# Second attention of a two-layer streaming encoder: keys on the partitions, maxima from a score pass of their own, query groups outside heads, output projection beside the next group

## The chip, the cores and the metric

One NeuronCore of one Trainium2 chip runs the whole program. The metric is the device time of one execution in microseconds (us), the median of several runs; lower is better. The engines are named as in the profile: PE (TensorE matmuls; PEld is its weight loads), DVE (VectorE), ACT (ScalarE), POOL (GpSimd) and SP (SyncE, which only issues DMAs here).

## The reference, cut to what matters

Two layers run on 2048 prompt tokens and 32 sample tokens, width 1024. Layer 0 (pooling mixer and sliding-window attention) and layer 1's input projection are the same before and after, but for the form in which layer 1's queries, keys and running sums are stored. What changes is layer 1's "forgetting attention" over the prompt (16 heads of 64) and the output projection behind it:

```python
cum_t = jnp.cumsum(logf, axis=1).transpose(0, 2, 1)          # running log-forget sums
bias  = ci[..., None] - cum_t[:, :, None, :]                 # c[query] - c[key]
s = jnp.einsum('nqhd,nkhd->nhqk', q, k) * ATTN_SCALE + bias  # per head, causal
p = jax.nn.softmax(jnp.where(mask, s, -jnp.inf), axis=-1)
out = jnp.einsum('nhqk,nkhd->nqhd', p, v)
y = x + (out * jax.nn.silu(gate)) @ w_out
```

Every product is computed to nearly fp32 accuracy by splitting an operand into a rounded part (hi) and the rest (lo). A split is two instructions: one engine rounds hi, another computes lo = value - hi.

## The kernel before, in words

The program is written in Python as one order of instructions. A planner then lays out each engine's stream ahead of time: it takes the written order as priority and an estimated timeline of when operands and buffers are ready, so an engine's stream can differ from the written order (matmuls of the output projection stand in PE's stream ahead of the last value products). At run time each engine works its own stream in order.

The stages: layer 0's projection, layer 0's attention with its output projection, layer 1's input projection with the sample's attention, and, as the last stage, the code of the change. There the loop runs over heads outside and over four groups I of 512 queries inside (`seq`).

`load_head` brings one head's operands for half of the tokens: qs (query hi over lo, 128 rows), ka (key hi over lo), kb (lo over hi) and vhl (value hi | lo) by POOL's DMA queue, and cb (the running sums, copied to all 128 partitions) by SP's.

`scores` has queries on the partitions. For each block of 128 queries and each piece of up to 1024 keys it issues two matmuls per 512 keys (ka, then kb: together all four hi/lo products), one small bf16 matmul for the causal mask, then one DVE instruction (L1053) that reads the scores in PSUM, adds cb, writes the sum to SBUF (pr) and returns the row's minimum (the scores are negated). ACT (L1058) takes the exponential of the whole row with the minimum as its bias and returns the row's sum.

`values` needs the probabilities with keys on the partitions, so PE transposes every 128x128 block (L1077) into PSUM (pt). The block is split: for three blocks of five ACT rounds hi from pt and DVE computes lo from pt (PSUM) and ph (SBUF); for two of five ACT copies pt to SBUF (pf), DVE rounds hi and POOL computes lo (`PM`, `PS`). Two matmuls per block (L1070) add vhl times ph and vhl times pl into pa. At the end of a group ACT copies one half of pa (L1093) and DVE adds the other (L1094).

`finish`, once per pair of heads and group, makes reciprocals of the row sums, transposes them, multiplies with the gate sg (DVE) and the result op (POOL, L1109), and stores to m1T by SP. `weave` spreads the next group's score pieces among a group's value blocks.

The output projection comes behind all heads: `load_wo` splits w_out's eight row tiles, `halves` loads 128 tokens of m1T and splits them, and `out1` (L1196) issues 2 x 24 matmuls of 512 columns per token tile, a DVE addition of the residual and a store.

Of the kernel before, what the change touches and what calls it, by code (L numbers as in the profile page):

```python
# [34 lines left out]
CW = 256  # L35


def f32(ap):
    return ap.bitcast(F32)
# [3 lines left out]
def hybrid_step_kernel(ctx: ExitStack, tc: tile.TileContext, *args):  # L43
# [34 lines left out]
    qT = dram([16, 2, HD, NTOK], "qT")  # L78
    kT = dram([16, 2, HD, NTOK], "kT")
# [3 lines left out]
    cT = dram([256, P], "cT")  # L83
# [21 lines left out]
    maskb = ctile([P, P], "maskb", BF16)  # L105
    with pool_of(name="setup", bufs=1) as setup:
# [4 lines left out]
        nc.vector.tensor_copy(maskb, mask)  # L111

# [24 lines left out]
    def rstd_bits(ss, np_, count):  # L137
        """as rstd_of, for one column and without a table: a first guess from the exponent's bits, then Newton"""
# [26 lines left out]
    def flush(n=0):  # L165
        """issue the stores that wait, but for the last n"""
# [4 lines left out]
    # ------------------------------------------------------------------  # L171
    # one layer's input projection, h^T held as exact hi/lo parts
    # ------------------------------------------------------------------
    class Proj:
# [13 lines left out]
        def at(self, which, tok, n):  # L188
            """hi (0) or lo (1) part of h^T for tokens [tok, tok + n): [P, KT, n]"""
# [59 lines left out]
        def prefetch(self, plan, fast=False):  # L249
            """the column groups in the order of use; the next one's weights are loaded ahead"""  # L250
# [49 lines left out]
        def turns(self, new=None):  # L300
            """the turn that waits, one step behind the arithmetic it needs"""
# [4 lines left out]
        def head_norm(self, src, np_, nh, gB, eng):  # L306
            """src: [np, nh, 64] (PSUM or SBUF) -> normalized, scaled tile [np, nh, 64]"""
# [13 lines left out]
    def turn(pt, ev, o, t0, h0, npair, dstT):  # L321
        """normalized heads [P, 2 token tiles, npair x 2 heads x 64] -> exact hi / lo parts, transposed"""
# [6 lines left out]
        for hh in range(2):  # L329
            for w in range(2):  # L330
                store(dstT[h0 + hh:h0 + 2 * npair:2, w, :, t0 * P:(t0 + 2) * P].rearrange("h d t -> d h t"),
                      f32(hl[hh * HD:(hh + 1) * HD, w]))
# [98 lines left out]
        # ALiBi with the chunk mask, keys = 128 before the tile and its own 128  # L431
# [11 lines left out]
        # the sample's keys, values and queries for the sliding window, hi / lo parts  # L443
# [123 lines left out]
    def out_proj(pp, pool, lhs, wo, xres, dst, n, eng):  # L567
        """lhs: for 128 tokens (hi, lo) APs [P, KT, 128]; for the sample one AP [P, KT, 64]"""
# [180 lines left out]
    # ------------------------------------------------------------------  # L749
    # layer 1, input projection  # L750
    # ------------------------------------------------------------------
    late = ctx.enter_context(pool_of(name="late", bufs=1))
    mhs = late.tile([P, KT, 2 * NS], F32R, name="mhs", tag="mhs")
    with ExitStack() as es:
# [38 lines left out]
        # log forget gates and their running sums  # L793
        with pool_of(name="lf", bufs=1) as lf:
# [28 lines left out]
            def running_sums(src_h, nt, dst, tag):  # L823
                """src_h: [P, 16, nt] with positions t*128+p; dst: DRAM [16*nt, 128]"""
# [13 lines left out]
                for j in range(0, n, P):  # L838
# [5 lines left out]
                    nc.sync.dma_start(dst[j:j + m, :], o)  # L844
# [411 lines left out]
```

## Time and profile before

| what | value |
|---|---|
| median of 3 runs | 2676.89 us (2674.86 to 2678.17) |
| profiled execution, its span | 2675.6 us |
| first score matmul of the changed stage | 1639.5 us |
| last value product; from here only the output projection | 2506.9 us |
| PE / DVE / ACT / POOL busy, whole span | 97% / 60% / 44% / 43% |

A busy time is the union of an engine's instructions. PE's instructions overlap each other (a matmul's recorded duration is longer than the distance to the next), so PE's rates are read from the chain of waits, where a run of matmuls stands as one piece with its count. The mean of a group of instructions is the recorded duration of one; back to back, DVE and ACT instructions overlap by about a tenth of a microsecond.

### The profile page before, as it was taken

What the parts mean: (1) busy time and instruction counts of PE and PEld (TensorE: products, weight loads), DVE (VectorE), ACT (ScalarE), POOL (GpSimd) and SP (SyncE); (2) the same over time, 40 slices, a digit from 0 to 9 for tenths busy, and PEclk for the clock granted to TensorE, in tenths of its full rate; (3) what the DMA queues carried; (4) which work ended last, traced back from release to release, by engine and by line L of the source; (5) the groups of instructions that cost most, each with busy time, mean ns of one, the idle gap of its engine ahead of it and who ended that gap; (6) DMA issues with size and microseconds to landing.
All of it is one profiled execution on the core that took longest, in us unless ns stands there. A gap on an engine that the chain in (4) does not pass through costs nothing. (4 is left out here: it accounts for less than half of the span.)

```text
span 2675.6 us, 47345 instructions
## 1 busy us (share of the span) xinstructions
PE 2586.7 (97%) x17259; PEld 2345.5 (88%) x17259; DVE 1604.6 (60%) x3847; ACT 1166.4 (44%) x2424; POOL 1149.9 (43%) x1583
## 2 busy tenths in 40 slices
PE   6999999799998999999999999999999999999999
PEld 6999999688887999999999998887888878877787
DVE  7650244778765115554553324889988988888521
ACT  5321111556554122222222114777777777777310
POOL 4454240455534434554554422555555555553100
PEclk9999999799998999999999999999999999999999
DMA  6342110976738443445555316544354455443642
GB/s 187 101 110 88 44 47 23 211 185 169 181 100 266 161 159 97 105 111 132 144 146 139 94 62 162 145 113 122 97 148 120 102 120 141 111 103 90 194 149 75
DMA packets 314120, 338.14 MB, mean 126 GB/s; under 512 B 32311, under 2 KB 263887, under 8 KB 313886
## 3 DMA queue, kind: packets, MB, share of 16 engines
q1 hardware_dynamic: 233550, 242.82, 31.6%
q0 software_dynamic: 76320, 87.98, 15.1%
q10 hardware_dynamic: 4016, 4.31, 0.5%
q8 instruction: 136, 2.23, 0.4%
q14 instruction: 98, 0.80, 0.1%
HBM read 203.05 MB, written 132.06 MB: 125 GB/s over the span
## 5 line engine op out<-in xcount | busy, mean ns | idle before, releaser
L271 PE MATMUL pm<-whl,h 128*128 128x256 f32 (+1 forms) x5760 | 713.7, 283 | 6.3 <-ACT h L155 3.1
L271 PEld LDWEIGHTS pm<-whl,h 128*128 128x128 f32 x5760 | 694.9, 190 | 7.9 <-ACT h L155 3.5
L296 PE MATMUL pm<-h,whl 128*128 128x384 f32 (+2 forms) x2880 | 472.3, 322 | 0.0
L296 PEld LDWEIGHTS pm<-h,whl 128*128 128x128 f32 x2880 | 455.3, 188 | 1.8
L158 POOL TENSOR_TENSOR pl<-pf,ph 128x512 fp32r<-128x512 f32 (+3 forms) x270 | 303.6, 1127 | 263.5 <-DVE ph L157 253.2
L1058 ACT ACTIVATE pr<-pr,mnf 128x128 f32<-128x128 f32 (+15 forms) x256 | 309.6, 1211 | 61.6 <-DVE mnf L1053 60.6
L1077 PE MATMUL pt<-ident,pr 128*128 128x128 f32 x2176 | 323.3, 274 | 5.5 <-DVE pl L158 5.4
L1077 PEld LDWEIGHTS pt<-ident,pr 128*128 128x128 f32 x2176 | 251.2, 141 | 39.3 <-DVE pl L158 11.4
L158 DVE TENSOR_TENSOR pl<-pt,ph 128x512 fp32r<-128x512 f32 (+3 forms) x436 | 261.4, 612 | 39.8 <-ACT ph L155 36.7
L1048 PE MATMUL ps<-ka,qs 128*128 128x512 f32 (+3 forms) x640 | 253.6, 397 | 16.9 <-DVE mnf L1053 15.9
L1053 DVE CUSTOM_DVE_ANT_0 pr<-ps,cb 128x1024 f32<-128x1024 f32 (+7 forms) x256 | 248.8, 981 | 17.9 <-PE ps L1049 9.2
L155 ACT CAST ph<-pt 128x512 fp32r<-128x512 f32 (+3 forms) x436 | 224.9, 529 | 60.9 <-PE pt L1077 44.0
L1070 PE MATMUL pa<-pl,vhl 128*128 128x512 f32 (+3 forms) x640 | 249.2, 395 | 2.3 <-POOL pl L158 2.3
L1070 PE MATMUL pa<-ph,vhl 128*128 128x512 f32 (+3 forms) x640 | 243.6, 383 | 3.8 <-DVE ph L157 3.2
L1049 PE MATMUL ps<-kb,qs 128*128 128x512 f32 (+3 forms) x640 | 228.8, 366 | 0.0
L1082 ACT COPY pf<-pt 128x512 f32<-128x512 f32 (+3 forms) x270 | 140.3, 523 | 66.9 <-PE pt L1077 63.9
L157 DVE CAST ph<-pf 128x512 fp32r<-128x512 f32 (+3 forms) x270 | 143.9, 537 | 35.8 <-ACT pf L1082 35.7
L577 PE MATMUL po<-wo,mh 128*128 128x512 f32 x512 | 162.9, 398 | 0.8 <-ACT mh L155 0.5
L1048 PEld LDWEIGHTS ps<-ka,qs 128*128 128x128 f32 x640 | 121.2, 189 | 46.5 <-DVE mnf L1053 30.3
L157 POOL CAST whl<-wst 128x256 fp32r<-128x256 f32 (+1 forms) x184 | 73.3, 420 | 186.3 <-PE pm L281 105.5
L242 POOL TENSOR_SCALAR wst<-wst,g1c 128x256 f32<-128x256 f32 (+1 forms) x120 | 115.5, 968 | 88.2 <-DMA wst<-in_w_in_dram 86.4
L311 DVE TENSOR_REDUCE ssh<-sq 128x8 f32<-128x512 f32 (+3 forms) x99 | 62.4, 630 | 137.3 <-ACT sq L309 137.2
(396 smaller groups left out, 4050.9 us busy)
## 6 DMA issues: line engine op xcount, KB each, us to landing
qT<-qhl SPq DMA_DIRECT2D x192, 128.0 KB, 2.4
qs<-qT POOLq DMA_DIRECT2D x48, 512.0 KB, 7.3
wst<-in_w_in_dram SPq DMA_DIRECT2D x168, 128.0 KB, 2.6
kT<-qhl SPq DMA_DIRECT2D x128, 128.0 KB, 2.4
ka<-kT POOLq DMA_DIRECT2D x32, 512.0 KB, 7.1
kb<-kT POOLq DMA_DIRECT2D x64, 256.0 KB, 9.0
cb<-cT SPq DMA_DIRECT2D x32, 512.0 KB, 9.6
vhl<-vH POOLq DMA_DIRECT2D x32, 512.0 KB, 4.7
```

The costliest lines, as they stand in the source:

```text
L155: nc.scalar.copy(hi, src)
L157: eng_hi.tensor_copy(hi, src)
L158: eng_lo.tensor_tensor(out=lo, in0=src, in1=f32(hi), op=ALU.subtract)
L271: nc.tensor.matmul(ps[:, j, :], a[:, kt, :], b[:, kt, :], start=(i == 0), stop=(i == 3 * KT - 1))
L296: nc.tensor.matmul(ps, a[:, kt, c:c + P], b[:, kt, :], start=(i == 0), stop=(i == 3 * KT - 1))
L577: nc.tensor.matmul(ps, a[:, kt, :], wo[kt][:, b, cs], start=(i == 0), stop=(i == 3 * KT - 1))
L1048: nc.tensor.matmul(ps[:, s0:s0 + m], lhs, ka[:, ks], start=True, stop=False)
L1049: nc.tensor.matmul(ps[:, s0:s0 + m], lhs, kb[:, ks], start=False, stop=not diag)
L1053: nc.vector.tensor_tensor_reduce(out=pr[:, c0:c0 + n], in0=ps[:, :n], in1=cb[:, :n], scale=1.0, scalar=mns[-1][:, 0:1] if mns else 3e38, o ...
L1058: nc.scalar.activation(pr[:, :L], pr[:, :L], AF.Exp, bias=mns[-1][:, 0:1], scale=-1.0, accum_out=sm)
L1070: nc.tensor.matmul(pa[:, r0 * P:], vhl[b], pp[:, r0:].rearrange("p r q -> p (r q)"), start=(b == 0 and i == 0), stop=(b == nkb - 1 and i = ...
L1077: nc.tensor.transpose(pt[:, r, :], prs[r][:, b * P:(b + 1) * P], ident)
```

## The change

The last stage is written anew; the stage before it stores other tensors for it.

- Stored operands: `qX` and `kX` have 132 rows per head: lo, hi, and four rows more. For keys these are -1, -1 and the running sum's hi and lo; for queries 0, 0 (later overwritten by the maxima) and 1, 1. The 68 rows from hi on (`KC`) thus give, in one matmul, hi x hi plus the running sums minus the row's maximum. 12 small DMAs write the constant rows and 32 the sums, in place of two of cT.
- The loop runs over query groups I outside and heads inside (`units`). Operands come in tiles of 512 tokens, all by SP: qc and kc (68 rows), qd and kd (128 rows), vhl. A tile counter (`room`) lets a load be issued only when a buffer is free, in two lists, ahead of use.
- `minima(n)`: a pass with queries on the partitions, one 68-row matmul per 512 keys, the mask, and a DVE minimum over up to 1024 scores read from PSUM. The four minima per query row are split, transposed by PE and copied by ACT into rows of qc. It runs one or two units ahead, in parts between the blocks of the current unit.
- `weigh(n, b)`: the scores again, with 128 keys on the partitions and up to 512 queries along the free axis: two matmuls (kd x qd, then kc x qc) and the mask into pt. ACT takes the exponential from pt into SBUF (pf). The split reads pf: ACT rounds hi, DVE computes lo. POOL adds pf to a running sum acc of the unit (for b > 0).
- `values` waits AVL = 3 blocks and issues the two value matmuls as before, one PSUM buffer pa.
- `finish`: the sums over keys are sums over partitions now: acc is split (ACT, POOL) and multiplied by a matrix of twos on PE (four matmuls of 512 columns), DVE takes the reciprocal of 128x512, POOL multiplies twice.
- The output projection of group I-1 is a generator (`beside`) stepped between the blocks of group I; only group 3's four token tiles come at the end.

```diff
+        def weigh(n, b):
...
+            pt = p_t.tile([P, G], F32, name="pt", tag="pt")
+            diag = b >= 4 * I
+            nc.tensor.matmul(pt[:, cs], d["kd"][c][:, ks], d["qd"][0][:, cs], start=True, stop=False)
+            nc.tensor.matmul(pt[:, cs], d["kc"][c][:KC, ks], d["qc"][0][:KC, cs], start=False, stop=not diag)
+            if diag:
+                nc.tensor.matmul(pt[:, r0 * P:(r0 + 1) * P], identb, maskTb, start=False, stop=True)
+            if b == 0:
+                pf = accs[n] = wk.tile([P, G], F32, name="acc", tag="acc", bufs=3)
+            else:
+                pf = wk.tile([P, G], F32, name="pf", tag="pf", bufs=3)
+            nc.scalar.activation(pf[:, cs], pt[:, cs], AF.Exp, scale=-1.0)
...
+            split(ph[:, cs], pl[:, cs], pf[:, cs], nc.scalar, nc.vector)
+            if b:
+                nc.gpsimd.tensor_tensor(out=accs[n][:, cs], in0=accs[n][:, cs], in1=pf[:, cs], op=ALU.add)
...
+        def minima(n):
...
+                        nc.tensor.matmul(ps[:, s0:s0 + w], d["qc"][0][:KC, r * P:(r + 1) * P],
+                                         d["kc"][(c0 + s0) // G][:KC, :w], start=True, stop=not diag)
...
+                    nc.vector.tensor_reduce(out=mn[:, r, i:i + 1], in_=ps[:, :m], axis=AX.X, op=ALU.min)
...
+        def finish(n):
...
+                split(ah, al, acc, nc.scalar, nc.gpsimd)
+                for i, x in enumerate((ah, al)):
+                    nc.tensor.matmul(den, twos[:, hh, :], x, start=(hh == 0 and i == 0), stop=(hh == 1 and i == 1))
...
+            nc.vector.reciprocal(rec, den)
+            nc.gpsimd.tensor_tensor(out=sg, in0=sg, in1=rec, op=ALU.mult)
+            nc.gpsimd.tensor_tensor(out=sg, in0=sg, in1=ops.pop((I, hp)), op=ALU.mult)
+            nc.sync.dma_start(m1T[hp * P:(hp + 1) * P, cs], sg)
...
+        def beside(I):
+
+            if I == 0:
+                yield from load_wo()
+                return
+            if I == 1:
+                yield from out1(mhs, x1[NTOK:NALL, :], yso, NS, one_bank)
+            yield from group_out(I - 1, one_bank)
```

## Rows read from the trace of the kernel before

**Rows 1.** The page: busy time of each engine.

```profile
PE 2586.7 (97%) x17259; PEld 2345.5 (88%) x17259; DVE 1604.6 (60%) x3847; ACT 1166.4 (44%) x2424; POOL 1149.9 (43%) x1583
```

**Rows 2.** Stretches of the stage: PE, PEld, DVE, ACT, POOL busy; clock, DMA share, GB/s.

```profile
2000.00:2300.00 300.00, 291.09 (x1819) 242.29 (x1818) 265.65 (x556) 227.00 (x430) 164.11 (x168) 1.00 0.48 119
...
2470.00:2510.00 40.00, 37.56 (x203) 28.74 (x202) 28.91 (x39) 21.38 (x34) 11.98 (x7) 1.00 0.65 209
2510.00:2676.00 166.00, 161.72 (x714) 133.59 (x712) 37.15 (x44) 12.81 (x13) 1.29 (x1) 1.00 0.38 125
```

**Rows 3.** The chain of waits in order of time: start, us, what.

```profile
2406.39 0.88 PE pt L1077 x8
...
2507.08 164.66 PE ps L1196 x726
```

**Rows 4.** PE in order of time: the stage's first scores and first value product.

```profile
1639.47 0.39 PE L1048 MATMUL ps<-ka,qs 128*128 128x128 f32 x2
...
1651.30 0.48 PE L1070 MATMUL pa<-ph,vhl 128*128 128x512 f32 x1
```

**Rows 5.** DVE by line, 1637 to 2510 us: count | busy us, mean ns | idle before.

```profile
L1053 DVE CUSTOM_DVE_ANT_0 pr<-ps,cb 128x1024 f32<-128x1024 f32 (+7 forms) x256 | 248.8, 981 | 17.9 <-PE ps L1049 9.2 <-PE ps L1051 3.3 <-PE pt L1077 3.1
...
L1053 DVE CUSTOM_DVE_ANT_0 pr<-ps,cb,mnf 128x128 f32<-128x128 f32 (+7 forms) x128 | 103.7, 810 | 8.0 <-PE ps L1051 5.3
...
L1102 DVE RECIPROCAL rr<-rs 128x8 f32<-128x8 f32 x32 | 6.3, 197 | 2.8 <-ACT pr L1058 2.8
```

**Rows 6.** DVE by line and form, from 1500 us.

```profile
L158 DVE TENSOR_TENSOR pl<-pt,ph 128x512 fp32r<-128x512 f32 x253 | 170.1, 683 | 23.5 <-ACT ph L155 22.3
...
L1094 DVE TENSOR_TENSOR op<-pa,tmp 64x512 f32<-64x512 f32 x64 | 43.8, 685 | 3.7 <-ACT tmp L1093 2.5
...
L1205 DVE TENSOR_TENSOR op<-ps,op 128x512 f32<-128x512 f32 x32 | 22.1, 691 | 117.3 <-PE ps L1196 117.3
...
L158 DVE TENSOR_TENSOR pl<-pt,ph 128x128 fp32r<-128x128 f32 x34 | 9.6, 283 | 2.1 <-ACT ph L155 2.0
```

**Rows 7.** POOL by line and form, from 1500 us.

```profile
L158 POOL TENSOR_TENSOR pl<-pf,ph 128x512 fp32r<-128x512 f32 x195 | 252.3, 1294 | 186.5 <-DVE ph L157 176.4 <-PE pt L1077 9.5
...
L158 POOL TENSOR_TENSOR pl<-pf,ph 128x128 fp32r<-128x128 f32 x30 | 14.8, 494 | 17.9 <-DVE ph L157 17.6
```

**Rows 8.** POOL in order of time: two of w_out's splits and a finish.

```profile
2478.29 2.40 POOL L158 TENSOR_TENSOR wo<-pr,wo 128x1024 fp32r<-128x1024 f32 x1
2480.65 2.27 POOL L1109 TENSOR_TENSOR sg<-sg,op 128x512 f32<-128x512 f32 x1
2482.87 2.40 POOL L158 TENSOR_TENSOR wo<-pr,wo 128x1024 fp32r<-128x1024 f32 x1
```

**Rows 9.** DVE in order of time, the same stretch.

```profile
2478.27 1.29 DVE L158 TENSOR_TENSOR pl<-pt,ph 128x512 fp32r<-128x512 f32 x2
2479.62 2.15 DVE L158 TENSOR_TENSOR wo<-pr,wo 128x1024 fp32r<-128x1024 f32 x1
2481.70 1.87 DVE L158 TENSOR_TENSOR pl<-pt,ph 128x512 fp32r<-128x512 f32 x3
2483.49 2.87 DVE L158 TENSOR_TENSOR pr<-pr 128x1024 fp32r<-128x1024 f32 x1
```

**Rows 10.** One line's instructions: count, duration ns min/median/max (L810, layer 1's gates).

```profile
L810 DVE RECIPROCAL ls<-ls x2: 233/982/1732, 1018.4 to 1021.8; 128x256 f32<-128x256 f32 x1, 32x16 f32<-32x16 f32 x1
```

**Rows 11.** ACT by line and form, from 1500 us.

```profile
L155 ACT CAST ph<-pt 128x512 fp32r<-128x512 f32 x253 | 144.6, 588 | 46.3 <-PE pt L1077 42.1 <-PE pa L1070 1.9
...
L1058 ACT ACTIVATE pr<-pr,mnf 128x512 f32<-128x512 f32 x16 | 11.7, 730 | 2.2 <-DVE mnf L1053 2.2
```

**Rows 12.** Who waited for whom: us in total, times, longest.

```profile
POOL sg L1109 <- DVE op L1094: 42.3, 24, 16.8
```

**Rows 13.** The page's DMA issues: count, KB each, us to landing.

```profile
m1T<-sg SPq DMA_DIRECT2D x32, 256.0 KB, 2.0
...
pr<-in_w_out_dram SPq DMA_DIRECT2D x8, 512.0 KB, 3.5
```

More of the change, by code (lines that the diff above doesn't have):

```diff
@@ L1112, in chain @@
-        def chain(gens):
-            for g in gens:
-                yield from g
-        def weave(main, n_main, side, n_side):
-            done = 0
-            for i, _ in enumerate(main):
-                want = n_side if i + 1 >= n_main else (i + 1) * n_side // n_main
-                while done < want:
-                    if next(side, 0) == 0:
-                        break
-                    done += 1
-            for _ in side:
-                pass
-        def n_chunks(I):
-            return sum(-(-(4 * I + r + 1) * P // SCH) for r in range(4))
@@ L1131, in hybrid_step_kernel @@
[L1131 to L1145 removed]
+        p_o = es.enter_context(pool_of(name="dpo", bufs=1, space=PSUM))
@@ new lines, in hybrid_step_kernel, with tile_of @@
+        nc.vector.memset(zero, 0.0)
+        turned = [fixed([P, 4, HD + 2], f"tm{i}", F32R) for i in range(2)]
+        for t in turned:
+            nc.vector.tensor_copy(t[:, :, 0:HD], zero)
+        units = [(I, h) for I in range(NG) for h in range(16)]
+        data = {}
+        BUFS = {"qc": 4, "kc": 9, "qd": 2, "kd": 5, "vhl": 5}
+        room = dict(BUFS)
+        def tile_of(tag):
+            room[tag] -= 1
+            return wk.tile([P, G], F32R, name=tag, tag=tag, bufs=BUFS[tag])
@@ new lines, in hybrid_step_kernel, with values @@
+        pas = {}
+        def values():
+            n, b, cs, ph, pl = waiting.pop(0)
+            I, h = units[n]
+            last = b == 4 * I + 3
+            if b == 0:
+                pas[n] = p_a.tile([P, G], F32, name="pa", tag="pa")
+            v = data[n]["vhl"][b // 4][:, b % 4 * P:(b % 4 + 1) * P]
+            for i, pp in enumerate((ph, pl)):
+                nc.tensor.matmul(pas[n][:, cs], v, pp[:, cs], start=(b == 0 and i == 0), stop=(last and i == 1))
+            if b % 4 == 3:
+                used("vhl")
+            if not last:
+                return
+            hp, hh = divmod(h, 2)
+            if hh == 0:
+                ops[I, hp] = wk.tile([P, G], F32, name="op", tag="op", bufs=2)
+            a, o = (slice(hh * HD, (hh + 1) * HD), slice((1 - hh) * HD, (2 - hh) * HD))
+            tmp = wk.tile([P, G], F32, name="tmp", tag="tmp", bufs=1)
+            nc.scalar.copy(tmp[a], pas[n][o])
+            nc.vector.tensor_tensor(out=ops[I, hp][a], in0=pas[n][a], in1=tmp[a], op=ALU.add)
+            del pas[n], data[n]
+            if hh == 1:
+                finish(n)
@@ new lines, in beside @@
+        def beside(I):
+            if I == 0:
+                yield from load_wo()
+                return
+            if I == 1:
+                yield from out1(mhs, x1[NTOK:NALL, :], yso, NS, one_bank)
+            yield from group_out(I - 1, one_bank)
+        BESIDE = [8, 48, 40, 40]
+        LATE = 6
+        prefetch()
+        ready = 0
+        for n in range(AHEAD):
+            for _ in minima(n):
+                pass
+            ready += 1
+        step = 0
+        side = beside(0)
@@ new lines, in hybrid_step_kernel @@
+        done = 0
+        for n, (I, h) in enumerate(units):
+            if h == 0 and I:
+                for _ in side:
+                    pass
+                side, done, step = beside(I), 0, 0
+            nkb = 4 * (I + 1)
+            todo = []
+            while ready < min(len(units), n + (AHEAD if I == 0 else 1) + 1):
+                todo.append(minima(ready))
+                ready += 1
+            parts = 0
+            total = sum(4 * (1 if 4 * units[ready - 1][0] + 4 <= 8 else 2) + 2 for _ in todo)
+            for b in range(nkb):
+                weigh(n, b)
+                prefetch()
+                want = total if b == nkb - 1 else min(total - 1, -(-(b + 1) * 4 * total // (3 * nkb)))
+                while todo and parts < want:
+                    if next(todo[0], 0) == 0:
+                        todo.pop(0)
+                        continue
+                    parts += 1
+                step += 1
+                if step > LATE:
+                    want2 = -(-(step - LATE) * BESIDE[I] // (16 * nkb - LATE))
+                    while done < want2:
+                        next(side, 0)
+                        done += 1
+            for g in todo:
+                for _ in g:
+                    pass
@@ L1226 @@
+        while waiting:
+            values()
+        for _ in side:
+            pass
+        for _ in group_out(NG - 1, two_banks):
+            pass
 _INS = ['x_prompt', 'x_sample', 'state_pool', 'cache_swa_k', 'cache_swa_v', 'cache_fox_k', 'cache_fox_v',
```

332 lines of the change are left out of this document (161 added, 171 removed).

## Prediction

> **What bounds the kernel now.** First the page's busy times: PE is busy 97% of the span, no other engine over 60% [rows 1]. Then the stretches: inside the stage PE works 291 of 300 us, DVE 266, ACT 227, POOL only 164, at the full clock, with DMA at half its share; behind it PE works almost alone [rows 2]. Then the chain of waits: in its tail 726 matmuls of 512 columns pass in 164.66 us, 0.227 each, and 8 transposes in 0.88 us, 0.11 each [rows 3]. With these two prices PE's work from the first score (1639.5 us [rows 4]) adds up. One "kind" of product (ka, kb, ph or pl) has, over 16 heads, 448 matmuls of 512 columns and 64 each of 384, 256 and 128: 448 x 0.227 + 64 x 0.341 = 123.5 us. Four kinds are 494, 2176 + 128 transposes 253, 256 masks at a quarter of 0.227 15, the output projection's 800 matmuls 182: 944 us, where 1032 pass up to the last matmul's end near 2671.7 (2507.1 + 164.7). PE bounds the stage; 88 us are turnarounds and short waits.
>
> **What the change does to PE.** Removed: 2176 transposes (239 us) and finish's 128 (14). Added: a fifth kind (the maxima, 123.5), 256 transposes (28), 128 matmuls of 512 for the sums (29), 256 masks (15; at most 59 if each took the 0.23 us that lies between two lone matmuls). Sum -58 us. Weaving the projection beside the next group moves PE's work and saves none of it. New PE total: 944 - 58 = 886 us. So if PE stayed the bound, the gain would be some 2%.
>
> **What it does to DVE and POOL.** This decides. Before, DVE's lo reads pt in PSUM and ph in SBUF; after, all 640 blocks read pf and ph, both in SBUF. POOL gets 576 additions acc + pf, both in SBUF, and 4 instructions of 512 in each of 32 finishes. The trace shows what happens when DVE reads two SBUF tensors beside POOL. On POOL two w_out splits of 1024 columns and a 512 multiplication follow each other [rows 8]; DVE does lo's from PSUM and two of 1024 columns from SBUF [rows 9]. The PSUM ones are not touched: two in 1.29 us, three in 1.87, with POOL in full work. The SBUF ones are: the first starts at 2479.62 and ends at 2481.77, 1.08 us after POOL's split ended (2480.69). POOL's multiplication, started at 2480.65, takes 2.27 instead of about 1.3 and ends at 2482.92, 1.15 after DVE. POOL's next split ends at 2485.27, DVE's next lo, started at 2483.49, at 2486.36, 1.09 after it. They take turns, and each end is one instruction behind the other's.
>
> Prices in turn: POOL 1.15 for 512; per column (1294 - 494)/384 = 2.08 ns [rows 7], so 0.88, 0.62 and 0.35 for 384, 256 and 128. DVE 1.08 for 1024; per column (683 - 283)/384 = 1.04 ns [rows 6], so 0.55, 0.42, 0.285, 0.15. Sums: additions (b > 0) 384 x 1.15 + 64 x 1.85 = 560; finishes 128 x 1.15 = 147; lo's 448 x 0.55 + 64 x 0.855 = 301; 20 lo's of 1024 for w_out and the woven token tiles 22. Together 1030 us in which one of the two holds what they share: more than PE's 886.
>
> Here the Trainium skill, SBUF — State Buffer, section "Who interferes with whom", goes further than the rows: it says that a DVE instruction with two SBUF inputs and a GpSimd one that reads SBUF exclude each other for the whole instruction. The turns agree that they exclude each other; of the length they show about 0.15 us less per POOL instruction than its duration. By whole durations the sum would be 1220 us: a rival below.
>
> DVE's own sum. The minima: 384 reductions over the same shapes as L1053's, at most 249 + 104 = 353 us [rows 5] (L1053 reads cb too; the bare reduction isn't shown, and 278,528 columns at 1.04 ns are 290; I take 353, the row of the same shape). Lo's 301, additions of pa 44, of residuals 23 [rows 6], the 1024 lo's 22. The reciprocal of 128x512: (1732 - 197)/248 = 6.2 ns per column [rows 5, 10], 3.3 us, x 32 = 106. Some 176 tiny ones at 0.2 [rows 5]: 35. Sum 884. To this come DVE's waits: it works in order, so behind a lo that waits for POOL stand the next minima and lo's, and PE waits for both. An addition becomes ready with the exponential, a lo one cast (0.59 [rows 11]) later, so a lo finds at most 1.15 - 0.59 = 0.56 us of an addition left, at least nothing. 640 x 0 to 0.56 is 0 to 358 us. Neither end has a row here; I take the middle, 179: 1063 us, just over the 1030 of the turns.
>
> ACT: 278,528 columns are 544 blocks of 512, at 0.59 for the cast and 0.59 to 0.73 for the exponential (without bias and row sum it lies between a cast and L1058 [rows 11]) 642 to 718, and some 200 copies 120: under 840, hidden.
>
> Finishes: a chain POOL, PE, DVE's reciprocal, POOL. While POOL's multiplication waits, additions behind it stand, and SP's store of m1T waits with the next loads behind it. Bounds: nothing (other blocks planned between) to 32 x (0.45 + 3.3) = 120; the nearest row is POOL's waiting for DVE before the same multiplication, 42.3 us [rows 12], now partly counted in DVE's sum: 20.
>
> At no cost: the 42 additional small stores in layer 1's projection on SP. PE's work there (rows 1: 97%) has its weights loaded a column group ahead; uncovered, one after the other at 2.0 us [rows 13], 84. POOL loses all its load issues, which weren't on the path. The loads by SP: per head 10 + 10 + 10 tiles of keys and values and 12 of queries, 8.2 MB, against 5.2; with gates, stores, w_out and residuals 178 MB, over 1150 us 155 GB/s against 119, and 209 is shown in this stage [rows 2]. Keys of the next unit are loaded while the present one works, so I count nothing; the early group is a rival.
>
> Start: first score 1639, then 12 us to the first value product [rows 4]; the new start has the same steps. Tail behind the last lo: value products, copy, addition, sums 2.2; reciprocal 3.3; two multiplications 2.6; store 2.0, load 3.5 [rows 13]; split 2.2; 192 matmuls at 0.227 43.6; addition and store 2.7: 62 us, against 168 now.
>
> **Sum.** 1639 + 12 + 1063 + 20 + 62 = 2796 against the span of 2675.6; the median is 1.3 above that span, so 2797 us: 4.5% slower. What is won on the tail is lost in the stage, where PE stands at 886/1075 of it.
>
> **Rivals.**
>
> *PE stays the bound.* The turns in rows 8 and 9 are few and between long instructions; if the planner sets POOL's additions where DVE reads PSUM (minima, pa, reciprocals: 526 us of DVE's work), little is lost and PE's sum counts: 2677 - 58 = 2619; without any idle 88 less, with dear masks 44 more. For it: PE is the bound now, and ACT, DVE and POOL all lie under 890 by themselves. Against it: additions and lo's sum to 1030 whatever their order. It decides if what DVE and POOL share stands under 2619 - 1639 - 12 - 20 - 62 - 1 = 885 us, 14% below my sum. Chance 0.20.
>
> *They hold it for whole durations.* POOL 384 x 1.294 + 64 x 2.24 + 128 x 1.294 = 806, DVE 448 x 0.683 + 64 x 1.24 + 27 = 412: 1218 us, no room for overlap, so 2797 + 155 = 2952. DVE's largest waits give the same (884 + 358 = 1242). For it: means of rows 6 and 7; against it: the ends in rows 8 and 9. This is what the Trainium skill's section says read literally. Chance 0.10.
>
> *The early group waits for loads.* In group 0 a unit has 1.6 MB to move (keys, values, queries, gate, store, w_out) in some 6.2 us, 258 GB/s. At the 209 shown it takes 7.7, 16 units 24 us more: 2821; at 119 it would be 2913. Chance 0.03.
>
> *No change.* The turns and the weave cancel, shared time near 943: 0.05.
>
> **Chances and range.** Forecast 0.62, its own range 2744 (turns alone, 1030, nothing for finishes) to 2886 (DVE's waits halfway to their largest). What can be told from no change is 0.2%, 5 us. Slower: 0.62 + 0.10 + 0.03 = 0.75; same 0.05; faster 0.20. For 8 in 10 the range reaches below into the first rival, to its value, and above to 2910: it leaves out half of that rival (0.10) and most of the second (0.07).
>
> **What will show it.** Right: lo's of 128x512 on DVE (pl from pf, ph) at 0.9 to 1.0 us in the mean instead of 0.683, additions on POOL over 1.3; DVE and POOL together over 90% in the stage while PE stands at 80 to 85%; the last attention work near 2734. In the chain of waits DVE's lo's and POOL's additions in place of PE. Wrong, if lo's keep 0.68 beside POOL's additions; if PE is over 95%; if PE's clock falls in the new gaps, which no row here prices; or if DVE is idle for long, with loads or pa named as releasers.

## The result, and the profile after

The changed kernel takes 3222.58 us (median of 4 runs, 3210.97 to 3232.29), 1.2034 times the kernel before (95% interval 1.2003 to 1.2064): 20% slower, where 4.5% was forecast and 2910 us was the upper end. The profiled execution spans 3215.6 us, 540 more than before.

The page after: PE, at 97% before [rows 1], stands at 89%, and TensorE's granted clock (PEclk, in tenths, 40 slices of the span) is mostly under 9 from slice 21 on, where the changed stage begins; before it was full there [rows 2].

```profile
PE 2866.1 (89%) x16235; PEld 2434.6 (76%) x16235; DVE 2011.9 (63%) x3581; ACT 1289.7 (40%) x2684; POOL 1631.2 (51%) x1816
...
PEclk9999998999899999999987698768877779888788
```

The stage as one stretch (columns as in [rows 2]):

```profile
1640.00:3160.00 1520.00, 1249.97 (x4783) 893.41 (x4781) 1207.03 (x1347) 791.56 (x1498) 942.68 (x704) 0.80 0.38 115
```

The tail came out as forecast (68 us from the last value matmul at 3147.3, for 62). Nearly all the rest is in the stage, where PE is busy 82% at a mean granted clock of 0.80, DVE 79%, POOL 62%.

For one measure across all kernels I took PE's matmuls from the first score to the last value matmul. The time from one start to the next is split into its columns at 2.4 GHz, one per cycle (at 1.2 GHz matmuls of 512 columns start 0.427 us apart, which is 512 cycles), what the half clock adds to these (up to as much again, where the matmul starts at 1.2 GHz), and the rest, called gaps: waits, and the few tens of ns between matmuls. Before: 867.6 us = 616.5 columns + 1.2 clock + 249.7 gaps. After: 1492.0 = 777.3 + 226.5 + 487.7. The columns are more because the woven projection came in from the tail; they are what was forecast. The gaps of the two aren't quite alike: 124 us of those before stand behind 2304 transposes, which start 109 ns apart for 53 ns of columns, and after has 256 transposes. Like for like some 126 us of gaps became 460.

The clock first. PE's stretches around some of its falls (PE busy, clock, DMA share, GB/s):

```profile
2407.70:2414.50 6.80, 5.44 (x19) 1.00 0.17 46
2414.50:2417.90 3.40, 3.40 (x11) 0.50 0.31 104
2417.90:2424.80 6.90, 3.73 (x21) 0.99 0.52 157
2424.80:2435.00 10.20, 10.20 (x29) 0.50 0.37 117
```

After a stretch with waits (5.44 of 6.80 us busy, 3.73 of 6.90) the clock goes to half; at half, in the stretches shown, PE works without a break and gets the full clock back; then it is ahead of the others again and waits. After 1640 us there are 70 stretches at half the clock, 615 us together. They aren't all like those shown: up to the last value matmul PE is busy 88% of the time at half the clock and 78% of the time at the full one. The Trainium skill (TensorE: Matmul & The Clock Gate, section "HAM oscillation — how this bites in real kernels") describes such a swing for a matmul loop that waits for its next load in each tile. The trace shows a swing too, but the waits are on DVE, ACT and DMA, and 244 of PE's 320 idle stretches are under a microsecond.

DVE by line and form (count | busy us, mean ns | idle before), against [rows 5, 6]:

```profile
L166 DVE TENSOR_TENSOR pl<-pf,ph 128x512 fp32r<-128x512 f32 x384 | 446.8, 1190 | 41.0 <-ACT ph L163 40.7
...
L1207 DVE RECIPROCAL rec<-pt 128x512 f32<-128x512 f32 x32 | 107.3, 3352 | 21.4 <-PE pt L1205 21.1
...
L166 DVE TENSOR_TENSOR pl<-acc,ph 128x512 fp32r<-128x512 f32 x64 | 44.1, 688 | 12.8 <-ACT ph L163 12.4
...
L165 DVE CAST tm<-mn 128x4 fp32r<-128x4 f32 x64 | 42.7, 668 | 0.5
```

The lo's of a unit's first block, before its additions begin, take 688 ns; the others of that shape 1190. Half of DVE's idle time (160 of 313 us) stands before the minima, for PE's scores (all widths in one row):

```profile
L1112 DVE TENSOR_REDUCE mn<-ps 128x1 f32<-128x1024 f32 (+7 forms) x384 | 343.3, 906 | 159.7 <-PE ps L1109 116.0 <-PE ps L1106 41.9
```

POOL's additions of the same shape, against [rows 7]:

```profile
L1157 POOL TENSOR_TENSOR acc<-acc,pf 128x512 f32<-128x512 f32 x384 | 585.0, 1523 | 363.4 <-DVE pl L166 252.9 <-ACT pf L1152 74.0 <-PE ps L1106 8.0
```

And lo's and additions in order of time, as in [rows 8, 9] (start, us), first DVE, then POOL:

```profile
2624.29 4.00 DVE L166 TENSOR_TENSOR pl<-pf,ph 128x512 fp32r<-128x512 f32 x3
...
2630.02 6.26 DVE L166 TENSOR_TENSOR pl<-pf,ph 128x512 fp32r<-128x512 f32 x4
```

```profile
2624.43 1.62 POOL L1157 TENSOR_TENSOR acc<-acc,pf 128x512 f32<-128x512 f32 x1 [0.20 <-ACT pf L1152]
2626.02 1.72 POOL L1208 TENSOR_TENSOR sg<-sg,rec 128x512 f32<-128x512 f32 x1
2627.69 1.74 POOL L1157 TENSOR_TENSOR acc<-acc,pf 128x512 f32<-128x512 f32 x1
...
2630.63 9.02 POOL L1157 TENSOR_TENSOR acc<-acc,pf 128x512 f32<-128x512 f32 x6
```

One lo for one addition, some 1.5 us for the pair: four lo's in 6.26 us, six additions in 9.02. The turns are there, but in a run of them DVE is held for nearly the whole pair, not for 0.55 and a part.

The same over the whole stage, sorted by whether a POOL instruction is under way when the DVE instruction starts: 312 of the 384 lo's of 128x512 meet one, take 1309 ns in the mean and end 0.55 us (the median) behind it; the other 72 take 677. POOL pays too: its 321 additions of 128x512 that overlap a lo take 1572 ns, the other 63 take 1276. The minima over 1024 scores, which read PSUM alone, take 1217 ns beside POOL and 1219 without it.

Who waits for whom between 1680 and 3050 us (us in total, times, longest):

```profile
PEld ps L1106 <- DMA kc<-kX: 90.8, 49, 4.3
PE ps L1106 <- DMA kc<-kX: 77.8, 48, 3.9
...
PEld pa L1176 <- DVE pl L166: 64.1, 94, 2.6
```

PE waits for key tiles, which the prediction counted at nothing; over the whole execution, from the page:

```profile
L1106 PE MATMUL ps<-kc,qc 68*128 68x512 f32 (+3 forms) x640 | 266.4, 490 | 135.0 <-DMA kc<-kX 91.3
```

The keys are loaded a unit ahead of where the text uses them; but the planner has moved the minima's matmuls up: PE takes those of unit 43 (a unit is one head of one query group, counted from 0) while unit 40 is at work (2409 to 2436 us), and the kc that it stops for at 2424.70 was issued at 2419.34.

### The profile page after: what moved, and what is told of

Same layout as the page of the kernel before. It is cut to its first block, busy times and chain, and to the rows that moved or that the text cites. A ratio compares the mean times of both kernels' runs of the same rounds, so it can differ in the third digit from the quotient of the medians.

```text
span 3215.6 us, 47649 instructions
## 1 busy us (share of the span) xinstructions
PE 2866.1 (89%) x16235; PEld 2434.6 (76%) x16235; DVE 2011.9 (63%) x3581; ACT 1289.7 (40%) x2684; POOL 1631.2 (51%) x1816
## 4 chain that ended last, share of the span: by engine, by line
PE 68%; DMA 13%; DVE 9%; issue 4%; POOL 3%; ACT 3%; SPq 0%; POOLq 0%; ACTq 0%; DVEq 0%
PE pm L279 20%; PE pm L304 14%; DMA kc<-kX 7%; PE pa L1176 5%; PE po L585 5%; PE ps L1106 4%; DVE pl L166 3%; PE po L1242 3%; PE pt L1144 3%; PE pt L1145 3%; POOL acc L1157 2%; DVE mn L1112 2%; DMA qc<-qX 2%; PE ps L1242 1%; PE pm L289 1%
## 5 line engine op out<-in xcount | busy, mean ns | idle before, releaser
L1157 POOL TENSOR_TENSOR acc<-acc,pf 128x512 f32<-128x512 f32 (+3 forms) x576 | 752.0, 1306 | 575.6 <-DVE pl L166 265.2
L166 DVE TENSOR_TENSOR pl<-pf,ph 128x512 fp32r<-128x512 f32 (+3 forms) x576 | 569.9, 1016 | 66.9 <-ACT ph L163 65.2
L1152 ACT ACTIVATE pf<-pt 128x512 f32<-128x512 f32 (+3 forms) x576 | 301.2, 525 | 432.3 <-PE pt L1145 160.1
L1112 DVE TENSOR_REDUCE mn<-ps 128x1 f32<-128x1024 f32 (+7 forms) x384 | 343.3, 906 | 159.7 <-PE ps L1109 116.0
L1106 PE MATMUL ps<-kc,qc 68*128 68x512 f32 (+3 forms) x640 | 266.4, 490 | 135.0 <-DMA kc<-kX 91.3
L1144 PE MATMUL pt<-qd,kd 128*128 128x512 f32 (+3 forms) x640 | 299.1, 467 | 39.4 <-ACT pf L1152 25.3
L163 ACT CAST ph<-pf 128x512 fp32r<-128x512 f32 (+3 forms) x576 | 308.8, 548 | 21.2 <-PE pa L1176 9.0
L1145 PE MATMUL pt<-qc,kc 68*128 68x512 f32 (+3 forms) x640 | 278.8, 436 | 0.0
L1144 PEld LDWEIGHTS pt<-qd,kd 128*128 128x128 f32 x640 | 153.7, 240 | 89.0 <-ACT pf L1152 47.9
L1176 PEld LDWEIGHTS pa<-ph,vhl 128*128 128x128 f32 x640 | 155.4, 243 | 40.2 <-DVE op L1187 13.0
```

The source lines that it names most:

```text
L163: nc.scalar.copy(hi, src)
L166: eng_lo.tensor_tensor(out=lo, in0=src, in1=f32(hi), op=ALU.subtract)
L1106: nc.tensor.matmul(ps[:, s0:s0 + w], d["qc"][0][:KC, r * P:(r + 1) * P], d["kc"][(c0 + s0) // G][:KC, :w], start=True, stop=not diag)
L1112: nc.vector.tensor_reduce(out=mn[:, r, i:i + 1], in_=ps[:, :m], axis=AX.X, op=ALU.min)
L1144: nc.tensor.matmul(pt[:, cs], d["kd"][c][:, ks], d["qd"][0][:, cs], start=True, stop=False)
L1145: nc.tensor.matmul(pt[:, cs], d["kc"][c][:KC, ks], d["qc"][0][:KC, cs], start=False, stop=not diag)
```

## The experiments

All ratios are to the kernel before on the same chip. The last three columns split the time between PE's matmul starts as above (us). "no adds" leaves POOL's additions out, "light" lets DVE's minimum read 128 scores; both take exponentials of a hundredth of the score (all of them, or the first block's) so that they stay in range, and don't compute the output.

| run | us | ratio, 95% | columns | clock | gaps |
|---|---|---|---|---|---|
| before | 2677 | | 617 | 1 | 250 |
| after | 3223 | 1.203 (1.200 to 1.206) | 777 | 227 | 488 |
| e1 no adds | 3116 | 1.163 (1.160 to 1.165) | 777 | 178 | 438 |
| e2 adds on DVE | 3273 | 1.223 (1.221 to 1.225) | 777 | 259 | 514 |
| e3 additional matmuls | 3187 | 1.191 (1.186 to 1.195) | 893 | 104 | 460 |
| e4 later load issue | 3201 | 1.197 (1.192 to 1.201) | 777 | 227 | 477 |
| e5 minima in order | 3227 | 1.205 (1.202 to 1.208) | 777 | 214 | 513 |
| e6 e5, no adds | 2942 | 1.099 (1.097 to 1.101) | 777 | 80 | 354 |
| e7 all of PE in order | 3236 | 1.208 (1.206 to 1.210) | 777 | 222 | 508 |
| e8 projection last | 3236 | 1.207 (1.202 to 1.211) | 711 | 264 | 490 |
| e9 minima, projection in order | 3174 | 1.185 (1.183 to 1.187) | 777 | 168 | 503 |
| e10 e9, no adds | 2942 | 1.098 (1.097 to 1.100) | 777 | 94 | 350 |
| e11 e10, light | 2887 | 1.078 (1.074 to 1.082) | 777 | 71 | 314 |
| e12 after, light | 3252 | 1.214 (1.212 to 1.216) | 777 | 269 | 488 |
| e13 e9, more buffers | 3368 | 1.257 (1.255 to 1.259) | 777 | 284 | 584 |
| e14 e13, no adds | 3046 | 1.137 (1.135 to 1.139) | 778 | 132 | 419 |
| e15 e9, light | 3083 | 1.151 (1.149 to 1.153) | 777 | 121 | 459 |
| e16 before, lo's on DVE twice | 2765 | 1.032 (1.031 to 1.034) | 624 | 3 | 334 |
| e17 e9, ACT's copies in order | 3248 | 1.213 (1.211 to 1.215) | 777 | 203 | 548 |
| e18 e17, no adds | 3085 | 1.153 (1.151 to 1.155) | 777 | 134 | 440 |

**e1: no additions.**

```diff
-            if b:
-                nc.gpsimd.tensor_tensor(out=accs[n][:, cs], in0=accs[n][:, cs], in1=pf[:, cs], op=ALU.add)
```

> Leaves out GpSimd's 576 additions of the exponentials into the running sum (and takes the first block's exponential of a hundredth of the score, so that its sum stays in range); everything else of the changed kernel stands. Theory 1, the shared port: the additions (752 us busy) and VectorE's 576 lo's (1016 ns each, 570 us) keep each other off the SBUF; without them the lo's fall to about 690 ns, the tiny subtractions of the minima to under 300 ns, TensorE runs without gaps at a granted clock above 0.97 in the stage, and the time comes to 2620 to 2800 us. Theory 2, loads: SyncE's queue is blocked at its head by loads that wait for buffers in the written order, and TensorE waits for kc; then the lo's get shorter but the stage stays over 1350 us and the time over 3050 us. Theory 3, the order of TensorE's work itself (matmul waits for exp, exp for matmul): lo's shorter, time 2850 to 3050 us, granted clock still under 0.9.

The lo's fell as expected (its page; 1016 ns in after, in the mean of the same four widths):

```profile
L166 DVE TENSOR_TENSOR pl<-pf,ph 128x512 fp32r<-128x512 f32 (+3 forms) x576 | 378.6, 684 | 132.2 <-ACT ph L163 129.5
```

So the sharing is shown. But only 107 us went, and the clock was still at half for 480 us: as a full explanation theory 1 fell here. The time lies where theory 2, the loads, had it. What goes with the additions is more than the sharing: ACT's waits for a pf that an addition still reads (29 us in after between 1680 and 3050), and the sums no longer come behind the last addition. No run takes the sharing away alone.

**e2: additions on DVE.**

```diff
-                nc.gpsimd.tensor_tensor(out=accs[n][:, cs], in0=accs[n][:, cs], in1=pf[:, cs], op=ALU.add)
+                nc.vector.tensor_tensor(out=accs[n][:, cs], in0=accs[n][:, cs], in1=pf[:, cs], op=ALU.add)
```

> The 576 additions are done by VectorE and not by GpSimd. Theory 1 (shared port): VectorE gets about 576 x 0.6 = 350 us more work but its lo's lose about 190 us of waiting, and its stage comes to 1200 to 1270 us against 1508 us: 2920 to 3020 us in all. Theory 2 (loads) and theory 3 (order of TensorE): the stage isn't set by the additions, and the time stays within 2% of 3222 us, or goes up with VectorE's 160 us more.

Slower than after by 1.6%, where theory 1 had 2920 to 3020 us. The lo's fell to 677 ns, but the additions took 363 us on DVE: relief from the sharing is no gain when the same engine takes the work.

**e3: the first matmul of each score block twice.**

```diff
+            nc.tensor.matmul(pt[:, cs], d["kd"][c][:, ks], d["qd"][0][:, cs], start=True, stop=True)
             nc.tensor.matmul(pt[:, cs], d["kd"][c][:, ks], d["qd"][0][:, cs], start=True, stop=False)
```

> The first matmul of each of the 640 score blocks is issued twice (the first one's output is overwritten): 640 more matmuls of up to 512 columns, about 145 us of TensorE's work at the full granted clock, 290 us at half. Theory of the clock (615 us of the stage ran at half the clock because TensorE had gaps; the gaps are set by the shared port): the added work lies in the gaps and keeps the clock up; the granted clock rises from 0.77 to 0.85 in the middle of the stage to over 0.9, and the time is 3050 to 3250 us, not slower. If TensorE's work is simply the bound at the clock it gets: 3222 + 145 to 290 = 3370 to 3510 us, with the granted clock as before.

More work on the busiest engine, and 35 us less time. The same stretch of e3 and of after:

```profile
1860.00:2160.00 300.00, 262.76 (x1217) 191.47 (x1218) 247.79 (x280) 164.24 (x320) 198.93 (x152) 0.96 0.43 132
```

```profile
1860.00:2160.00 300.00, 254.79 (x998) 182.75 (x998) 222.36 (x251) 150.47 (x291) 179.17 (x139) 0.79 0.40 122
```

The time is in the range of the theory of the clock. Columns +116, clock -123, gaps -27: only 27 of the 116 us went into the gaps; the rest was paid for by the clock that came back (0.96 in this stretch for 0.79).

**e4: loads issued four blocks later** (kc, kd, qc and qd likewise; `freed` is counted down once per block).

```diff
-                used("vhl")
+                freed.append(("vhl", 4))
```

> A load into a buffer is issued four score blocks later than the buffer's last reader in the written order, so that SyncE's queue is less often blocked at its head by a load whose buffer is still in use. Theory 2 (loads): TensorE's waits for kc and qc (135 us before the minima's matmuls) fall by more than half and the time by 70 to 130 us, to 3090 to 3150 us. Theory 1: the waits for kc fall, but the shared port still sets the pace, and the time stays within 40 us of 3222 us. If the loads have too little lead already, the waits for kc grow and the time goes over 3260 us.

22 us less, but the two intervals overlap. The waits for kc stayed (94 and 79 us, for 91 and 78): the edit left the loads as late as they were, and the 70 to 130 us of theory 2 didn't come.

**e5: the minima's matmuls where they are written; e6: the same without additions.**

```diff
-                        nc.tensor.matmul(ps[:, s0:s0 + w], d["qc"][0][:KC, r * P:(r + 1) * P],
+                        tc.keep_in_program_order(nc.tensor.matmul(ps[:, s0:s0 + w], d["qc"][0][:KC, r * P:(r + 1) * P],
```

> Only the order of TensorE's stream is changed: each matmul of the minima's pass stays behind the matmuls written before it (one unit ahead of use), where the changed kernel's stream has it up to three units ahead, right where its kc load lands. Theory of the order: the stream stops at these matmuls for loads issued 2 to 6 us before (135 us for kc and qc), and the gaps cost the clock too; now the waits for kc and qc before line 1106 fall under 30 us, the time at half the clock from 615 us to under 400 us, and the time to 2920 to 3090 us. Rival, the stage is paced by the exponentials, lo's and additions: the waits only move to the score and value matmuls, and the time stays within 60 us of 3222 us.

> The order of the run above and no additions by GpSimd (they are left out, with the first block's exponential of a hundredth of the score, as in the first experiment). If late loads by order and the shared port are the two causes and the clock follows from their gaps: TensorE's own 886 us at a clock over 0.95, 2620 to 2800 us in all. If a third cause of gaps is as large (the way of a block from score through exp, cast and lo to the value matmul with two score banks): over 2900 us, with waits for exp and lo and the clock still under 0.93.

In e5 no wait for loads is left among the large ones, and nothing is won, as the rival had it: PE waits for lo's in their place.

```profile
PEld pa L1176 <- DVE pl L166: 188.6, 235, 3.5
```

Without additions the same order takes 173 us off (e1 to e6). Late loads and the additions are two covers of one another: mending either gives 0 or 107 us, both 280. It isn't all; e6 is 2942, not 2620 to 2800: the third cause that its forecast named (over 2900 us) is there.

**e7: all of PE's stream in order** (the wrapper of e5 around each matmul of the stage)**; e8: the projection behind the attention.**

```diff
-            yield from group_out(I - 1, one_bank)
+            return
...
-        for _ in group_out(NG - 1, two_banks):
-            pass
+        for I in range(NG):
+            for _ in group_out(I, two_banks):
+                pass
```

> All matmuls of the stage stay in the written order: score of block b, values of block b-3, a part of the next unit's minima, a part of the projection. Theory of the order: waits for loads vanish as in the minima's order alone, and no value matmul is taken ahead of its lo: 2850 to 3050 us. Against it: at a unit pair's end the two sums' matmuls then stand in the stream where they are written, behind GpSimd's last addition and lo (3 to 5 us, 32 times, 100 to 160 us), so that the time comes out above the run with the minima's order alone, 3050 to 3250 us.

> The output projection isn't woven into the next group; all of it stands behind the attention (its 576 matmuls of 512 columns woven before, 131 us at 0.227, are moved). Theory that the weave fills gaps which would be there anyway: the attention ends where it did or 60 us earlier at most, and the time is 3260 to 3350 us, the clock in the stage lower than 0.81. Theory that the woven matmuls delay scores and values in TensorE's stream: the attention ends 131 us earlier or more, 3150 to 3222 us in all.

e7: the sums' matmuls wait, as feared, for ACT's cast (74 us before their weight loads) and POOL's lo (69). e8: the planner still set half of the projection into the attention, all of it behind 3020 us; 66 us of columns less ended it only 27 us earlier (3120.7 for 3147.3), since the clock lost 38 us more. So most of what the woven matmuls cost in columns they gave back in clock; the time, 3236, stays just under the first theory's range.

**e9, e10: projection in order too. e11: light minima. e12: light minima alone.**

```diff
-                        nc.tensor.matmul(ps[:a.shape[2]], a[:, kt, :], wo[kt][:, j, cs], start=(i == 0),
+                        tc.keep_in_program_order(
+                            nc.tensor.matmul(ps[:a.shape[2]], a[:, kt, :], wo[kt][:, j, cs], start=(i == 0),
...
-                    nc.vector.tensor_reduce(out=mn[:, r, i:i + 1], in_=ps[:, :m], axis=AX.X, op=ALU.min)
+                    nc.vector.tensor_reduce(out=mn[:, r, i:i + 1], in_=ps[:, m - P:m], axis=AX.X, op=ALU.min)
```

> Minima and output projection both stay in TensorE's stream where they are written; in the changed kernel and with the minima's order alone, most of a group's 192 projection matmuls stand in the first three units of the next group (their units take 35 to 43 us each, with VectorE at 60 to 75%), and the other units take 33 us with VectorE 87% busy. Theory, two bounds in turn (TensorE in the first three units, VectorE with its lo's held by GpSimd in the rest): spread evenly the projection hides under VectorE, about 25 us less in each of three groups, 3130 to 3170 us. Rival, TensorE at the clock it gets paces all units: its work is the same, 3200 to 3250 us.

> The same order, and GpSimd's additions left out as before. With the minima's order and no additions (2942 us) the first three units of a group took 74, 95 and 109 us where the later ones take 46, 56 and 70 us per three. Theory of the two bounds in turn: spread evenly about 100 us go, 2820 to 2870 us, with VectorE over 88% busy in the stage. If TensorE alone bounds once the shared port is gone: 2620 to 2720 us. Rival without bunching: within 40 us of 2942 us.

> As the run before, and VectorE's minimum reads only the last 128 of up to 1024 scores (all exponentials are taken of a hundredth of the score, so that they stay in range): about 230 us less of VectorE's work, nothing less of TensorE's. Theory that VectorE is the bound left when the additions are gone: TensorE becomes the bound at a clock over 0.97, 2640 to 2730 us. Rival, the path of a block (score, exp, cast, lo, values) or TensorE's own order: less than 50 us faster than the run before.

> The changed kernel with nothing but VectorE's minimum reading the last 128 of up to 1024 scores (and exponentials of a hundredth of the score): about 230 us less of VectorE's work; additions, order and loads stand. Theory that VectorE with its held lo's paces the stage: 150 to 230 us faster, 2990 to 3070 us. Rival, TensorE's stream waiting for loads is a pace of its own, as it was when the additions alone were left out (107 us faster): 3100 to 3180 us. If neither: within 40 us of 3222 us.

e9 took 52 us off e5, a little less than the two bounds in turn gave; e10 took nothing off e6, against it. From e9 to e10 the additions are worth 233 us: 153 of gaps, 74 of clock, 6 elsewhere. In e11 DVE, with some 230 us less to do, isn't a bound any more (busy 62% from 1640 to 2820 us), and yet only 54 us went, far from 2640 to 2730. e12 is the sharpest miss: the same relief with the additions, and the time goes up by 30. A stretch of it:

```profile
2400.00:2800.00 400.00, 339.25 (x1214) 242.87 (x1214) 259.55 (x334) 205.22 (x383) 248.77 (x183) 0.79 0.35 108
```

DVE is busy 65%, PE 85% at 0.79: PE still stops at the loads (93 us before its weight loads, 75 before its matmuls) and loses more by the clock (269 us for 227), so what DVE saves is not used. Part of it is lost again at once: the lo's take 629 us for 570.

**e13, e14: four score banks, more tiles on the way, values four blocks behind. e15: e9 with light minima. e16: the kernel before, DVE's lo's made twice** (the last line of the diff)**.**

```diff
-        p_t = es.enter_context(pool_of(name="dpt", bufs=2, space=PSUM))
+        p_t = es.enter_context(pool_of(name="dpt", bufs=4, space=PSUM))
...
-        SCH = 1024
-        AVL = 3
+        SCH = 512
+        AVL = 4
...
                     split(ph[:, r0:], pl[:, r0:], pt[:, r0:], nc.scalar, nc.vector)
+                    nc.vector.tensor_tensor(out=pl[:, r0:], in0=pt[:, r0:], in1=f32(ph[:, r0:]), op=ALU.subtract)
```

> The order of the ninth run, and more room for a block on its way: four score banks instead of two (the minima's tiles become one bank each, 512 scores per reduction), five exponential tiles instead of three, seven hi and lo tiles instead of five, values four blocks behind instead of three. Theory of the short way: TensorE's waits for exponentials and lo's (about 400 us in the ninth run) go down by half, the time at half the clock from 494 us to under 250 us, and VectorE's sum with held lo's (about 1240 us) is what is left: 2980 to 3080 us. Rival, VectorE and GpSimd pace it already and room changes nothing: 3130 to 3200 us.

> The same room, and GpSimd's additions left out (first block's exponential of a hundredth of the score, as before). Against the tenth run (2942 us). Theory of the short way: with neither the shared port nor the few buffers TensorE's own 886 us bound the stage at a clock over 0.98: 2650 to 2780 us. Rival, something else keeps TensorE from its pace: over 2880 us.

> The order of the ninth run (3174 us) with its additions, and VectorE's minimum over the last 128 of up to 1024 scores (exponentials of a hundredth of the score): 230 us less of VectorE's work. If VectorE with held lo's paces the stage once loads are out of the way: 2980 to 3060 us. If the pace is TensorE's at the clock that its gaps leave it, as the twelfth run suggests: within 60 us of 3174 us, with the time at half the clock not under 450 us.

> The kernel before, with the lo that VectorE makes of a block (from PSUM and SBUF) made twice, about 320 instructions and 200 us of VectorE's work more: VectorE's 266 of 300 us become about 330, so it is the bound by a tenth and TensorE gets gaps of some 12%. Theory of the clock (gaps bring the clock to half wherever they come from): the time at half the clock rises from 6 us to 200 us or more, and the time to 2850 to 3000 us. If the clock doesn't follow from gaps alone: VectorE's sum, 2740 to 2820 us, under 60 us at half the clock.

e13 and e14 went the wrong way, by 193 and 104 us: ACT, in order, waited 265 us in e13 (107 in e9) at the copy of a unit's result and 166 (73) at the copy of the minima, and the next unit's exponentials stood behind them. That these waits are the cause isn't shown; the edit has several parts. e15: with the loads in time DVE's 230 us are worth 92 (in e12 nothing), between its two forecasts; the minima fell from 340 to 103 us, but the lo's, meeting more additions, rose from 587 to 656. e16 bounds the clock theory: DVE is the limit, PE has gaps, the clock stays.

```profile
2000.00:2300.00 300.00, 278.18 (x1666) 219.71 (x1667) 291.63 (x630) 214.09 (x394) 148.50 (x154) 1.00 0.42 106
```

Of its 202 idle stretches of PE (76 us in all, 7 us at half the clock) 12 are over 1 us; in after 76 of 320 are, 150 of 257 us. So gaps alone don't bring the clock down. But the length of the waits isn't the whole of it either: e11 has no more than 20 over 1 us (105 us idle in all), and the clock is at half in 28 stretches, 191 us. What sets e11 apart from e16 stays open.

**e17, e18: ACT's two copies where they are written.**

```diff
-            nc.scalar.copy(tmp[a], pas[n][o])
+            tc.keep_in_program_order(nc.scalar.copy(tmp[a], pas[n][o]))
...
-            nc.scalar.copy(d["qc"][0][HD:HD + 2, :], pt[HD:HD + 2, :])
+            tc.keep_in_program_order(nc.scalar.copy(d["qc"][0][HD:HD + 2, :], pt[HD:HD + 2, :]))
```

> The ninth run, and ScalarE's two copies of a unit (of its result from pa, of its minima into qc) stay in ScalarE's stream where they are written, three blocks into the next unit, and not ahead of that unit's exponentials. Theory of the drained unit (the stream's order lets a unit run dry before the next starts, some 4 us in each of 64 units): ScalarE's waits at these two copies fall from 180 us to under 60 us, VectorE's wait for casts from 104 us to under 60 us, and the time from 3174 us to 3040 to 3110 us. Rival, VectorE with held lo's is the pace and the drained ends lie beside it: within 30 us of 3174 us.

> The same order, and GpSimd's additions left out (first block's exponential of a hundredth of the score). Against the tenth run (2942 us). Theory of the drained unit: 2800 to 2870 us. Rival, the units' ends cost nothing beside VectorE's sum, 85% of the stage there: within 30 us of 2942 us.

Slower by 73 and 143 us, against both theories. In e17 the wait at the copy of the result is gone from the list, that at the copy of the minima has grown from 73 us to 176, and the sums' matmuls wait instead:

```profile
ACT qc L1126 <- PE pt L1125: 175.8, 47, 8.4
...
PEld pt L1205 <- ACT ph L163: 99.7, 29, 4.7
```

No run beat the kernel before. The best that computes everything is e9, 48 us under the change.

## Why the prediction was wrong

The direction and the mechanism that the prediction chose were right: DVE and POOL hold each other up over SBUF, and POOL's additions are the largest single cause found (107 us alone, 233 to 284 with the loads in time). The size was wrong. Forecast for the profiled span: 2796, measured 3215.6. In the split above the forecast's stage, 1639 to 2734, was 777 columns and 318 gaps, with no term for the clock. Of the 420 us between, the clock is 227, gaps 170, the start 16, the tail 6. Seen from DVE, the bound engine of the forecast, the stage was to be 1063 us of its work and waits for POOL, and 20 us of pauses; it was 1207 and 313. The two accounts are of the same time, and the points below overlap: they don't add up to 420.

- **The step that failed: a stage that lasts as long as DVE's 1063 us, in which PE "stands at 886/1075 of it" and what PE loses costs nothing.** DVE does not work without pauses, and that PE at 82% keeps the full clock was assumed; "if PE's clock falls in the new gaps, which no row here prices" stood among what would make it wrong, with no rival and no width of the range for it. The split puts the clock at 227 us; e3, where 123 of them came back, bears it out, but no run takes the clock's fall away alone. [rows 2] couldn't show it: PE was busy 97% there.
- **"DVE's own sum 884", and waits at "the middle, 179".** The lo's took 570 + 44 = 614 us against 301 + 179 = 480. The price in turn was right: a lo ends 0.55 us behind POOL's instruction. The wait before it was not: the prediction had at most 0.56 us of an addition left, and the 312 lo's of 128x512 that met a POOL instruction found 0.83 us in the mean. Additions follow one another, as in the stretch shown, so that a lo often meets one that has just begun. POOL's turn was dearer in the forecast: 1.70 us for the pair, measured 1.5 in a run of them. The tiny instructions took 100 us for 35. The minima (343 for 353) and reciprocals (107 for 106) were right.
- **"Keys of the next unit are loaded while the present one works, so I count nothing."** 135 us of waits for keys and queries in PE's stream, by the planner's order. Taken away by themselves they are worth nothing (e5), beside the additions' removal 173 (e6).
- **"Finishes 20".** DVE is idle 313 of 1520 us, 160 of them before the minima, for PE's scores. Waits go round through four in-order streams, and which of them holds is different after each edit (e7, e13, e17).
- **The rivals.** PE as the bound failed with additions and, at 2942 us, without them. Whole durations, 2952, was the nearest, and that is luck: the lo's and additions share less than that (a pair 1.5 us, alone 0.68 and 1.28), and the rest of its distance is pauses and clock, which it didn't have either.

Of its own signs for the sharing, lo's of 0.9 to 1.0 us were 1.19 and additions over 1.3 were 1.52. Two of those that it had set down against itself came too: the clock fell, and DVE was idle for long.

Open: what holds the kernel at 2942 us when additions and late loads are both gone (350 us of gaps, some 330 without those behind transposes, against 126 before, and 94 of clock). It isn't DVE's work (e11). The ends of the units are a likely place, but the edits there (e13 and e14, e17 and e18) didn't show it.

## What to carry to other kernels

When a change takes PE from nearly always busy to four fifths, give the clock its own term: it cost 227 us here, 71 in e11 and 3 in e16, all with waits in PE's stream, and what decides between them stays open. When the other side of a shared path has its work queued back to back, count a wait as the greater part of one whole instruction of it, not as what is left over on average. Before trusting one bound, ask what order the planner will give: it lays out streams for times that the change itself makes untrue, and mending one wait showed the next.

## What the hardware showed beside this

The tiny VectorE instructions are caught by the sharing too, and not only those with two inputs: `mn` to `tm`, a cast of 128x4 with one input, took 668 ns in the mean in after and, in e10,

```profile
L165 DVE CAST tm<-mn 128x4 fp32r<-128x4 f32 x64 | 11.4, 179 | 0.4
```

The 668 is a mean of two kinds: 36 of the 64 casts start while a POOL instruction is under way, take 1060 ns and end 26 to 35 ns behind it; the other 28 take 164. The Trainium skill (SBUF — State Buffer, section "Who interferes with whom") has casts among the instructions that can take the shared ports; the trace agrees with these numbers.

Additional matmuls made a kernel faster: 116 us of columns more, 35 us (1.1%) less time (e3).
